# An 8 KB transfer ahead of gamma's load in an RMSNorm-and-swish kernel

## The chip, the cores and the metric

The kernel runs on one core of one Trainium2 chip. The metric is the device time of one execution in microseconds. Most executions of a kernel agree within a few tenths of a per cent; all executions compared below are of the fast state unless it is said otherwise, and the granted clock was 1.0 in every profile. "Slow" here means only that an execution took over 1.5% more than the fastest of the same kernel.

## The reference

```python
x: (16, 1024, 512) float32, gamma: (512,) float32, eps = 1e-5
rms    = np.sqrt(np.mean(x ** 2, axis=-1, keepdims=True) + eps)
x_norm = x / rms * gamma
return x_norm * (1.0 / (1.0 + np.exp(-x_norm)))
```

33.6 MB are read and 33.6 MB written.

## The kernel before

x is cut into 11 tiles of 128 partitions by 4 to 16 rows, worked on in 32 chunks of four rows. A ring of 96 rows in SBUF holds x, and the result replaces x in place. SP issues all loads, ScalarE all stores and gamma's load.

```python
sizes = [4, 4, 8] + [16] * 6 + [8, 8]
...
nc.gpsimd.memset(gamma4, 0.0).then_inc(s_zero, 1)
...
need(
    nc.scalar.dma_start(out=gamma4[0:P:32, :], in_=gamma.partition_broadcast(4)),
    s_zero, 1,
).then_inc(s_gld, 16)
nc.scalar.preload_act_table_set("silu_and_others")
stored = 0
for k in range(K + 3):
    if k < K:
        square(k)                    # ScalarE, two instructions
    while stored < T and ends[stored] <= k - 2:
        store(stored)
        stored += 1
    if 2 <= k < K + 2:
        swish(k - 2)                 # ScalarE, in place
...
for k in range(K + 1):               # VectorE
    if k < K:
        sums(k)                      # reduction of the squares
    if k == 0:
        need(nc.vector.stream_shuffle(gamma_sb, gamma4, [0] * 32), s_gld, 16
        ).then_inc(s_gamma, 1)       # gamma to all partitions
    if k == 1:
        nc.vector.wait_ge(s_gamma, 1)
    if k >= 1:
        norm(k - 1)                  # four multiplies by rstd and gamma
```

GpSimd adds eps and takes the power -0.5 between `sums` and `norm`.

## Time and profile before

| | before |
|---|---|
| median time | 160.29 us (160.28 to 160.62, 3 runs) |
| span in the profile | 160.0 us (that execution took 161.31 us) |
| VectorE / ScalarE / GpSimd busy | 87% / 78% / 41% |
| moved by DMA | 67.14 MB, 420 GB/s over the span |

### The profile page before, as it was taken

Reading aid. Unit: us, or ns where it says so; the run is one execution under the profiler, and the core shown is the slowest. Engines: PE = TensorE matmul, PEld = TensorE weight load, DVE = VectorE, ACT = ScalarE, POOL = GpSimd, SP = SyncE. Lnnn points to the kernel's source line nnn. Section 1 sums busy time; section 2 is a strip of 40 time slices with the busy share of each in tenths; the row PEclk is TensorE's granted clock in tenths of the full one; section 3 lists DMA queues with packets and bytes.
Section 4 is the critical chain, followed back from the end, with each engine's and each line's share of the span. In section 5 each row is a group of like instructions: output and inputs, shape, how many; then the busy total and the mean of one; then the engine's idle time right before and its main releaser. Section 6 shows DMA issues by size and latency. Waiting matters only on the chain.

```text
span 160.0 us, 437 instructions
## 1 busy us (share of the span) xinstructions
DVE 139.1 (87%) x162; ACT 125.1 (78%) x129; POOL 65.5 (41%) x70
## 2 busy tenths in 40 slices
DVE  0298986999999999999999999999999999999100
ACT  1839849888888889988888888888899888884400
POOL 1043552444555555444444445555554444444000
DMA  6999999989999999999999999999999999999994
GB/s 250 444 487 393 393 381 455 475 358 477 426 408 442 414 483 395 418 483 410 401 461 451 393 442 459 401 451 442 426 393 455 414 442 442 467 401 405 430 434 180
DMA packets 3179, 67.14 MB, mean 420 GB/s; under 512 B 356, under 2 KB 356, under 8 KB 360
## 3 DMA queue, kind: packets, MB, share of 16 engines
q1 hardware_dynamic: 1584, 33.56, 49.3%
q10 hardware_dynamic: 1592, 33.56, 48.8%
q14 instruction: 3, 0.02, 0.0%
HBM read 33.56 MB, written 33.55 MB: 419 GB/s over the span
## 4 chain that ended last, share of the span: by engine, by line
DVE 77%; DMA 13%; ACT 2%; issue 0%; SPq 0%; ACTq 0%
DVE xb L215 48%; DVE ms L204 29%; DMA xb<-in_x_dram 13%; ACT xb L178 1%; ACT sq L166 1%; ACT junk L159 0%; SPq L118 0%; ACTq L158 0%
## 5 line engine op out<-in xcount | busy, mean ns | idle before, releaser
L215 DVE SCALAR_TENSOR_TENSOR xb<-xb,rstd,gamma_sb 128x512 f32<-128x512 f32 x128 | 87.4, 747 | 0.0
L178 ACT ACTIVATE xb<-xb 128x2048 f32<-128x2048 f32 x32 | 61.1, 1908 | 16.3 <-DVE xb L215 16.3
L204 DVE TENSOR_REDUCE ms<-sq 128x3 f32<-128x1536 f32 x32 | 56.1, 1754 | 9.7 <-ACT sq L166 9.6
L141 POOL TENSOR_SCALAR aeps<-ms 128x4 f32<-128x4 f32 x32 | 20.7, 646 | 75.9 <-DVE ms L204 75.9
L166 ACT ACTIVATE sq<-xb 128x1536 f32<-128x1536 f32 x32 | 45.9, 1433 | 0.0
L148 POOL TENSOR_TENSOR rstd<-aeps,neg_half 128x4 f32<-128x4 f32 x32 | 44.0, 1376 | 2.7
L159 ACT ACTIVATE junk<-xb 128x512 bf16<-128x512 f32 x32 | 19.7, 615 | 5.7 <-DMA xb<-in_x_dram 5.7
L159 ACT ACTIVATION_READ_ACCUMULATOR junk<-xb 128x1 f32 x32 | 6.0, 187 | 0.0
L190 ACT ACT_TABLE_LOAD x1 | 1.3, 1283 | 3.6 <-issue 3.6
L136 POOL MEMSET gamma<- 128x512 f32 x1 | 0.5, 526 | 1.5 <-POOLq L65 1.5
L228 DVE STREAM_SHUFFLE gamma_sb<-gamma 128x512 f32<-128x512 f32 x1 | 0.7, 720 | 0.0
L255 POOL MEMSET const-float32-0.0<- 128x1 f32 x1 | 0.1, 99 | 0.2 <-issue 0.2
L255 POOL MEMSET const-bfloat16-1.0<- 128x1 bf16 x1 | 0.1, 103 | 0.0
L255 POOL MEMSET const-uint8-127<- 128x1 uint8 x1 | 0.1, 102 | 0.0
L137 POOL MEMSET neg_half<- 128x4 f32 x1 | 0.1, 102 | 0.0
L255 POOL MEMSET const-float32-1.0<- 128x1 f32 x1 | 0.1, 99 | 0.0
L228 DVE LOAD_MASK_SELECT gamma_sb<-gamma x1 | 0.0, 15 | 0.0
## 6 DMA issues: line engine op xcount, KB each, us to landing
xb<-in_x_dram SPq DMA_DIRECT2D x6, 4096.0 KB, 44.5
out_dram<-xb ACTq DMA_DIRECT2D x6, 4096.0 KB, 29.8
xb<-in_x_dram SPq DMA_DIRECT2D x3, 2048.0 KB, 38.5
out_dram<-xb ACTq DMA_DIRECT2D x3, 2048.0 KB, 11.3
xb<-in_x_dram SPq DMA_DIRECT2D x2, 1024.0 KB, 5.9
out_dram<-xb ACTq DMA_DIRECT2D x2, 1024.0 KB, 19.8
gamma<-in_gamma_dram ACTq DMA_DIRECT2D x1, 8.0 KB
```

What stands on the lines that cost most here:

```text
L136: nc.gpsimd.memset(gamma4, 0.0).then_inc(s_zero, 1)
L137: nc.gpsimd.memset(neg_half, -0.5).then_inc(s_half, 1)
L141: nc.gpsimd.tensor_scalar(out=aeps[:, k, :], in0=ms[:, k, :], scalar1=eps_f, scalar2=None, op0=ALU.add,),
L148: nc.gpsimd.tensor_tensor(out=rstd[:, k, :], in0=aeps[:, k, :], in1=neg_half, op=ALU.pow),
L159: acc = nc.scalar.activation(out=junk[k % 2], in_=xb[:, at + n_sq, :], func=AF.Square, scale=inv_d**0.5, accum_out=ms[:, k, n_sq : n_sq + 1],)
L166: square = nc.scalar.activation(out=sq[k % 2][:, 0:n_sq, :], in_=xb[:, at : at + n_sq, :], func=AF.Square, scale=inv_d**0.5,)
L178: nc.scalar.activation(out=rows, in_=rows, func=AF.Silu), s_norm, k + 1
L190: nc.scalar.preload_act_table_set("silu_and_others")
L204: nc.vector.tensor_reduce(out=ms[:, k, 0:n_sq], in_=sq[k % 2][:, 0:n_sq, :], op=ALU.add, axis=mybir.AxisListType.X,),
L215: ins = nc.vector.scalar_tensor_tensor(out=row, in0=row, scalar=rstd[:, k, j : j + 1], in1=gamma_sb, op0=ALU.mult, op1=ALU.mult,)
L228: nc.vector.stream_shuffle(gamma_sb, gamma4, [0] * 32), s_gld, 16
L255: nc = _bacc.Bacc("TRN2", target_bir_lowering=False, num_devices=1)
```

## The change

A transfer of 128 rows of 64 B from SBUF to a scratch tensor in HBM goes out from ScalarE's queue ahead of gamma's load. Nothing reads what it writes; SP waits for it at its end. As an optimization it has no purpose in the result: it puts something small in front of a load that VectorE needs early.

```diff
+    scratch = nc.dram_tensor("scratch", [P, 16], fp32, kind="Internal").ap()
+    blank = sbuf("blank", [P, 16])
...
     for t in range(early, T):
         load(t)
+    nc.sync.wait_ge(s_scratch, 16)
...
+    nc.gpsimd.memset(blank, 0.0).then_inc(s_blank, 1)
     nc.gpsimd.memset(gamma4, 0.0).then_inc(s_zero, 1)
...
+    need(nc.scalar.dma_start(out=scratch, in_=blank), s_blank, 1).then_inc(
+        s_scratch, 16
+    )
     need(
         nc.scalar.dma_start(out=gamma4[0:P:32, :], in_=gamma.partition_broadcast(4)),
```

More of the change, by code (lines that the diff above doesn't have):

```diff
@@ L81 @@
     st = [nc.alloc_semaphore(f"st{t}") for t in range(T)]
+    scratch = nc.dram_tensor("scratch", [P, 16], fp32, kind="Internal").ap()
+    blank = sbuf("blank", [P, 16])
+    s_blank = nc.alloc_semaphore("s_blank")
+    s_scratch = nc.alloc_semaphore("s_scratch")
     s_gld = nc.alloc_semaphore("s_gld")
```

## The prediction

> **What bounds the kernel now.** I read the page first (busy shares, the 40 slices), then the chain of waits, then the timeline of the first 27 us, the DMA view in narrow windows, and last the tail.
>
> From the page of the kernel before (busy time; tenths busy per fortieth of the span; the chain that ended last):
>
> ```profile
> DVE 139.1 (87%) x162; ACT 125.1 (78%) x129; POOL 65.5 (41%) x70
> ...
> DMA  6999999989999999999999999999999999999994
> ...
> DMA packets 3179, 67.14 MB, mean 420 GB/s; under 512 B 356, under 2 KB 356, under 8 KB 360
> ...
> DVE xb L215 48%; DVE ms L204 29%; DMA xb<-in_x_dram 13%; ACT xb L178 1%; ACT sq L166 1%; ACT junk L159 0%; SPq L118 0%; ACTq L158 0%
> ```
>
> The chain says: loads up to 23 us, then VectorE without a break to 148.8 us, then the last swish and a store. Taken alone that makes VectorE the bound. The DMA row says something else: it is full from the second slice to the last but one. 67.14 MB in about 157 us is 428 GB/s, and the 32 KB packets take 1.213 us each, which is 16 x 32,768 B / 1.213 us = 432 GB/s at best. So the transfers have almost no idle time either. The two meet at the end, where the second view (busy per stretch) shows the engines done and the stores still draining:
>
> ```profile
> 148.00:152.00 4.00, 0.80 (x2) 2.00 (x2) 0.00 (x0) 1.00 1.00 430
> 152.00:154.00 2.00, 0.00 (x0) 0.00 (x0) 0.00 (x0) 1.00 1.00 426
> 154.00:156.00 2.00, 0.00 (x0) 0.00 (x0) 0.00 (x0) 1.00 1.03 442
> 156.00:158.00 2.00, 0.00 (x0) 0.00 (x0) 0.00 (x0) 1.00 0.81 344
> ```
>
> (The last two columns are the DMA share and GB/s.) The last store is issued at 150.77 us and its packets start at about 152.7 us, right behind those of the store before it. The end is thus set by the drain of the stores, and compute has a little slack before it.
>
> The start, from the timeline (start, duration, engine, line):
>
> ```profile
> 1.90 0.53 POOL L136 MEMSET gamma<- 128x512 f32 x1 [1.48 <-POOLq L65]
> ...
> 2.46 1.08 ACTq L187 DMA_DIRECT2D gamma<-in_gamma_dram  x1
> 3.58 1.28 ACT L190 ACT_TABLE_LOAD   x1 [3.58 <-issue]
> ...
> 8.66 0.72 DVE L228 STREAM_SHUFFLE gamma_sb<-gamma 128x512 f32<-128x512 f32 x1
> ...
> 12.39 0.63 ACT L159 ACTIVATE junk<-xb 128x512 bf16<-128x512 f32 x1 [2.96 <-DMA xb<-in_x_dram]
> ...
> 25.25 1.76 DVE L204 TENSOR_REDUCE ms<-sq 128x3 f32<-128x1536 f32 x1 [2.04 <-ACT sq L166]
> ```
>
> Up to 25.25 us all waits are for x, and VectorE is then busy to the end. The shuffle that needs gamma comes second on VectorE, so a late gamma holds everything behind it.
>
> **What the Trainium skill says.** (1) "DMA: Bandwidth & Descriptors", section "Queues, rings and completion order": each DMA engine takes turns between the queues that have work, a packet at a time. The trace agrees: in 20 to 24 us the DMA view counts 50 packets of the load queue and 50 of the store queue, though the first are 32 KB and the second 8 KB. (2) Same page, "Why a DMA increments its semaphore by 16 and not by 1": a transfer with 128 partitions is spread over 16 engines, one with four rows over four. The trace agrees: the 356 packets under 512 B are 22 big transfers x 16 + 4 for gamma. (3) Same page, "Specifications": below 512 B a transfer costs a read-modify-write; no packet here tests that, since the only ones so small are semaphore updates (9 ns each). (4) "Perfetto Trace Analysis", section "DMA Instruction — HWDGE (DVE, Sync)": the profiled time of an issue doesn't hold the data movement. The trace agrees, and this matters here. Gamma's issue is 2.46 to 3.54 us, but no packet of its queue (q10) runs before 6.67 us:
>
> ```profile
> q1 hardware_dynamic: 66, 0.54, 127.7%
> q10 hardware_dynamic: 2, 0.00, 0.6%
> ...
> q1 hardware_dynamic: 25, 0.41, 95.5%
> q10 hardware_dynamic: 3, 0.01, 1.6%
> ...
> q1 hardware_dynamic: 23, 0.38, 87.8%
> q10 hardware_dynamic: 3, 0.00, 0.2%
> ```
>
> (windows 6 to 7, 7 to 8 and 8 to 9 us: packets, MB, share of 16 engines). The four 2 KB packets start at 6.67 to 7.56 us and the four semaphore updates at 6.76 to 8.25 us. On three engines a 16 KB load packet (0.61 us) stands between data and update. The first store shows the same 4.1 us from issue (16.31) to first packet (20.39). The x tile's last update at 6.95 us frees ScalarE at 7.37, so I add 0.4 us: gamma was usable at about 8.65 us, the moment the shuffle began.
>
> **The change, part by part.** Nothing is removed; the rest of each engine's order stays.
>
> POOL: one memset of 128x16, about 0.1 us (the 128x4 one took 102 ns), ahead of gamma's. Off the path.
>
> ScalarE's queue: one more issue. It needs only the small memset, so it starts at about 2.05 us. Issues took 1.08 us (gamma) and 0.34 to 0.36 us (stores). Gamma's own issue then moves from 2.46 to 2.5 to 3.1 us, and table load and first square by 0.1 to 0.7 us. ScalarE idles 0.42 us before chunk 1 and 2.96 us before chunk 2 waiting for x, so that is absorbed.
>
> SP: a wait for the scratch transfer, but after its last load issue (79.9 us). The transfer is over by then. Zero.
>
> DMA engines: 128 rows of 64 B plus 16 semaphore updates, 144 packets, nine per engine. 2 KB took 84 ns and 8 KB 309 ns, so about 37 ns per KB over some 9 ns: 64 B is about 11 ns (estimate from those two), 0.1 us per engine. As the end is a DMA drain, 0.1 us can show.
>
> Gamma's landing: this is the part with size. Gamma stands behind nine scratch packets in the same queue, and each takes a turn against a load packet. With the 4.1 us delay from issue, the first scratch packet comes at about 6.2 us, up to 6.7 us. Tile 2's load (16 KB packets, eight per engine) fills 6.65 to 11.9 us. One or two turns pass at the end of tile 1, the other seven or eight cost 0.61 us each: 4.3 to 4.9 us. The scratch update runs at about 10.5 to 11.5 us; gamma's data one turn later; its update another turn later, at 0.61 us or, if tile 3's 32 KB packets have begun, 1.22 us a turn. Gamma lands between 12.1 and 14.7 us (with the 0.4 us); call it 13.5, 4.8 us later than now.
>
> What that does on VectorE: from gamma's landing G to the start of chunk 4's reduction (25.25 us now) lie shuffle 0.65, three reductions of 1.67 and three groups of four multiplies of 2.65 (the steps in the chain): 0.65 + 5.0 + 7.95 = 13.6 us. It starts late only if G exceeds 25.25 - 13.6 = 11.6 us. With G = 13.5 VectorE runs 1.9 us late, for the rest of the kernel (0.5 to 3.1 us for the range of G).
>
> What that does to the end: the last store is issued at 150.77 + d. First load packets began 1.0 to 2.05 us after the first issue; with 2.05, then eight 16 KB packets (4.9 us) and 0.4 us, the end is 158.1 + d. Now it is 160.0, set by the drain (one DMA engine finishes at 159.64 us by my chaining of packets, the rest by 158.3). So d up to 1.9 us is hidden; 3.1 us would show 1.2 us. Loads aren't harmed: they wait in a full queue, tile 9's load is issued 22 us before its packets start.
>
> Sum: 0 to 1.2 us from gamma, some 0.2 us from packets and drain. 160.29 + 0.3 = 160.6 us.
>
> **The rivals.** First, all of VectorE's delay shows, as the chain of waits suggests: d of 0.5 to 3.1 us gives 160.8 to 163.4 us. For: VectorE has no gap after 25.25 us. Against: DMA is at 1.00 in the stretch in which VectorE stops. Second, gamma is hardly delayed: the 4.1 us may be a start-up of the queue which both transfers share, or small rows may travel together in one packet; then G is about 9 and the time is 160.3 to 160.4 us. For: no packet below 2 KB except updates is in this trace, so I can't see how 64 B rows are packed. Against: big rows go strictly one packet each. Third, the 64 B writes are slow to complete and gamma's update waits for them: G of 16 to 17, d about 5, 163 us or more. For: the page's remark on small writes. Against: nothing in this trace.
>
> Faster would need stores that start later to let the loads finish earlier, or the one late DMA engine to lose its 1.4 us; the bytes stay the same, so at most 1%.
>
> **Range and chances.** 2% is 3.2 us: it needs d above 5.1 us with the drain hiding 1.9, or the first rival at its upper edge. I give slower 0.05, faster 0.01, same 0.94. The range 160.1 to 162.0 us holds the main line and rival two whole, and a part of rivals one and three.
>
> **What would show it.** 500 packets under 512 B instead of 356 (128 + 16 more), the shuffle at 12 to 15 us with idle VectorE before it, chunk 4's reduction at 26 to 28 us, and a last store issued 0.5 to 3 us later while the span grows by less. A shuffle near 9 us would refute the turns; a span that grows by as much as the last issue moves would refute the slack in the drain; a shuffle after 16 us would mean that small writes cost more than turns.

## The result, and the profile after

The changed kernel took 160.12 us (median of 4 runs, 160.02 to 160.16), the kernel before 160.28 us in the same rounds. The ratio is 0.9985, with a 95% interval of 0.9968 to 1.0003. A ratio here is the mean time of one kernel's fast runs over that of the other's of the same rounds, so it isn't quite the ratio of the medians. The times are thus the same within their scatter; what there is of a difference points the other way from the predicted +0.3 us.

From the page of the changed kernel (busy time, DMA row, packets, the chain that ended last):

```profile
span 158.7 us, 439 instructions
...
DVE 138.9 (87%) x162; ACT 125.3 (79%) x129; POOL 65.4 (41%) x71
...
DMA  7999999999999999999999999999999999999997
...
q10 hardware_dynamic: 1736, 33.57, 49.3%
...
DVE xb L224 53%; DVE ms L213 32%; DMA gamma<-in_gamma_dram 5%; ACT xb L184 1%; DVE gamma_sb L237 0%; POOL gamma L142 0%; POOL blank L141 0%; POOLq L65 0%
```

ScalarE's queue (q10) has 1,736 packets instead of 1,592: 144 more, exactly 128 rows and 16 semaphore updates, so each row is a packet of its own. In the chain, gamma's load has taken the place of the x loads. Whoever reads only the chain sees a kernel that now hangs on gamma, and it isn't slower.

The start of the changed kernel, from the timeline (start, duration, engine, line):

```profile
2.04 0.35 ACTq L192 DMA_DIRECT2D scratch<-blank  x1
...
2.50 1.10 ACTq L196 DMA_DIRECT2D gamma<-in_gamma_dram  x1
...
11.04 0.72 DVE L237 STREAM_SHUFFLE gamma_sb<-gamma 128x512 f32<-128x512 f32 x1
...
18.01 0.34 ACTq L189 DMA_DIRECT2D out_dram<-xb  x1
...
22.39 0.63 ACT L165 ACTIVATE junk<-xb 128x512 bf16<-128x512 f32 x1
...
24.59 1.75 DVE L213 TENSOR_REDUCE ms<-sq 128x3 f32<-128x1536 f32 x1
```

The shuffle begins at 11.04 us instead of 8.66, after 2.26 us in which VectorE waited for gamma. The first store is issued at 18.01 us instead of 16.31. Tile 3 of x is there when ScalarE wants it at 22.39 us (no wait in front of that line), where it had waited until 23.15 us before. The reduction of chunk 4, from which on VectorE has no gap, begins at 24.59 us instead of 25.25: earlier, though gamma came later.

The DMA view of the changed kernel, 5.7 to 6.7 us and then 9.4 to 10.8 us (packets, MB, share of 16 engines):

```profile
q1 hardware_dynamic: 48, 0.39, 92.7%
q10 hardware_dynamic: 48, 0.00, 3.3%
...
q1 hardware_dynamic: 33, 0.54, 90.0%
q10 hardware_dynamic: 8, 0.01, 1.7%
```

48 load packets and 48 scratch packets in the same microsecond: strict turns, though one kind has 8 KB and the other 64 B. The packet records give the rest. A scratch packet takes 11 ns. On one DMA engine they start at 5.76, 6.08, 6.39, 6.70, 6.7 to 6.8, 7.33, 7.94 and 8.56 us, the update at 9.17 us; gamma's four packets start at 9.85 to 10.0 us and their updates at 10.54 to 10.69 us.

### The profile page after: what moved, and what is told of

It reads as the page before. It is cut to its first block, busy times and chain, and to the rows that moved or that the text cites. A ratio compares the mean times of both kernels' runs of the same rounds, so it can differ in the third digit from the quotient of the medians.

```text
span 158.7 us, 439 instructions
## 1 busy us (share of the span) xinstructions
DVE 138.9 (87%) x162; ACT 125.3 (79%) x129; POOL 65.4 (41%) x71
## 3 DMA queue, kind: packets, MB, share of 16 engines
q10 hardware_dynamic: 1736, 33.57, 49.3%
## 4 chain that ended last, share of the span: by engine, by line
DVE 85%; DMA 5%; ACT 1%; issue 1%; POOL 0%; POOLq 0%
DVE xb L224 53%; DVE ms L213 32%; DMA gamma<-in_gamma_dram 5%; ACT xb L184 1%; DVE gamma_sb L237 0%; POOL gamma L142 0%; POOL blank L141 0%; POOLq L65 0%
```

## The experiments

Two theories were put up for what sets the time. **D**: the transfers do. All bytes have to pass 16 DMA engines that are hardly ever idle, and compute has a little slack before the last store. **V**: VectorE does, as the chain of waits says, so the time moves one for one with the start of its unbroken run (chunk 4's reduction, from which on VectorE has no gap). For what delayed gamma there were three: turns in the queue, the bytes, or slow small writes to HBM.

### The changed kernel once more: after_again

No edit.

> The changed kernel once more, for a tighter interval and a second profile. Theory D (the drain of the transfers sets the end): 159.9 to 160.4 us, within 0.3 us of the kernel before, shuffle again at about 11.0 us. Theory V (the start of VectorE's unbroken run sets the end; it moved from 25.25 to 24.59 us): about 159.6 us, 0.65 us less than before.

Measured: 160.19 us (160.02 to 160.64, 6 runs), ratio 0.9989 (0.9968 to 1.001). Shuffle at 11.20 us, unbroken run from 24.96 us, last store issued at 150.49 us. As D expected; V's 159.6 us did not come. But with the start at 24.96 us, as in this profile, V would ask for only 0.3 us less than before, so this run doesn't separate the two. The profiled execution took 160.64 us, and in it one DMA engine ended at 158.94 us and the others by 158.24. That is worth keeping: in the profile before, one engine ended at 159.64 us and the others by 158.27 (161.31 us); in the first profile after, all ended by 158.30 (160.02 us). (I assigned packets to engines by chaining each start to the nearest end.) The scatter between executions is largely one late DMA engine: each of these three executions took 1.7 us longer than the time at which its last engine ended.

### Scratch behind gamma: behind

```diff
-    need(nc.scalar.dma_start(out=scratch, in_=blank), s_blank, 1).then_inc(s_scratch, 16)
     need(nc.scalar.dma_start(out=gamma4[0:P:32, :], ...), s_zero, 1).then_inc(s_gld, 16)
+    need(nc.scalar.dma_start(out=scratch, in_=blank), s_blank, 1).then_inc(s_scratch, 16)
```

> Scratch transfer issued behind gamma's instead of ahead. Both theories: shuffle back at about 8.7 us and the first store's issue back at about 16.3 us, since gamma no longer stands behind nine packets. D: 160.0 to 160.4 us, like the changed kernel. V: about 0.65 us more than the changed kernel, 160.3 us, as the unbroken run starts at about 25.2 us again. If the small writes themselves cost, this is slower than the kernel before by the same as the changed kernel.

Measured: 160.39 us (160.14 to 160.91), ratio 1.0000 (0.9976 to 1.0024). Shuffle at 9.08 us (right behind the first reduction, which ScalarE's extra issue had pushed to 7.40 us), first store at 16.20 us, unbroken run from 25.16 us. The start is that of the kernel before again, with the same 144 extra packets: the packets themselves cost nothing that shows.

### The same 8 KB in 16 rows: one_turn

```diff
-    scratch = nc.dram_tensor("scratch", [P, 16], ...); blank = sbuf("blank", [P, 16])
+    scratch = nc.dram_tensor("scratch", [16, 128], ...); blank = sbuf("blank", [16, 128])
```

> The same 8 KB ahead of gamma, but as 16 rows of 512 B: one data packet and one semaphore update on each DMA engine instead of eight and one. If the turns delay gamma: two turns instead of nine, gamma limited by its own issue again, shuffle at 8.7 to 9.3 us. If the bytes or the write to HBM delay it: shuffle at about 11 us as in the changed kernel. Time under D 160.0 to 160.4 us.

Measured: shuffle at 8.81 us, 160.49 us (160.26 to 160.81), ratio 1.0005 (0.9985 to 1.0026).

```profile
8.81 0.72 DVE L237 STREAM_SHUFFLE gamma_sb<-gamma 128x512 f32<-128x512 f32 x1
```

The same bytes, the same direction, ahead of gamma all the same, and gamma isn't late. Turns, not bytes.

### The rows read instead of written: read_in

```diff
-    need(nc.scalar.dma_start(out=scratch, in_=blank), s_blank, 1)
+    need(nc.scalar.dma_start(out=blank, in_=xf[0:P, 0:16]), s_blank, 1)
```

> The 128 rows of 64 B run the other way, from x in HBM into SBUF: no small write to HBM, the same nine packets a DMA engine ahead of gamma. If turns delay gamma: shuffle at 11.0 to 11.3 us as in the changed kernel. If the small write to HBM (read-modify-write, late confirmation) does: shuffle well before that, 9 to 10 us. Time 160.0 to 160.4 us either way.

Measured: shuffle at 11.12 us, 160.13 us (159.98 to 160.38, 4 runs), ratio 0.9988 (0.9959 to 1.0017).

```profile
11.12 0.71 DVE L236 STREAM_SHUFFLE gamma_sb<-gamma 128x512 f32<-128x512 f32 x1
```

Reads of 64 B do to gamma what writes of 64 B do, 11 ns a packet in both. Slow small writes are out.

### The first store one step later, no scratch: late_store and late_store_again

```diff
-        while stored < T and ends[stored] <= k - 2:
+        while stored < T and ends[stored] <= k - (3 if stored == 0 else 2):
```

> The kernel before without scratch, only the first store moved one step later in ScalarE's order (issue at about 22.5 to 23.5 us instead of 16.3). If the first store's packets are what slowed tile 3's load, that load lands at about 21.7 us, ScalarE's wait ends near 22.1 us and VectorE's unbroken run starts at about 24.2 us instead of 25.25. V: about 1 us faster than before, 159.2 us. D: no change, 160.0 to 160.4 us, since the same bytes have to drain.

Measured: tile 3's wait ends at 22.06 us, unbroken run from 24.16 us, both as expected; last store issued at 149.68 us; 159.89 us (159.81 to 160.48), ratio 0.9977 (0.9955 to 0.9999). The start, first of the kernel before and then of late_store:

```profile
16.31 0.36 ACTq L183 DMA_DIRECT2D out_dram<-xb  x1
...
23.15 0.63 ACT L159 ACTIVATE junk<-xb 128x512 bf16<-128x512 f32 x1 [2.32 <-DMA xb<-in_x_dram]
```

```profile
22.06 0.63 ACT L159 ACTIVATE junk<-xb 128x512 bf16<-128x512 f32 x1 [1.26 <-DMA xb<-in_x_dram]
...
24.16 1.76 DVE L204 TENSOR_REDUCE ms<-sq 128x3 f32<-128x1536 f32 x1 [0.98 <-ACT sq L166]
```

So a first store that doesn't take turns against tile 3's load does let that load land a microsecond earlier. Of V's 1 us some 0.4 us showed: V's 159.2 us is missed by 0.7, but D's "no change" (160.0 us at the least) is missed too, by 0.1.

> The kernel with the late first store and no scratch once more, to see if it beats both kernels. If its gain is real: ratio to before 0.996 to 0.999 again, about 159.9 us. If it was the draw of runs: 0.999 to 1.001.

Measured: 159.90 us (159.79 to 160.08), ratio 0.9966 (0.9948 to 0.9984). This version beats the kernel before in two sets of runs, by 0.2 to 0.3%. The changed kernel ran beside it only in the first (after_again), with a mean of 160.24 us against 160.04, which the scatter of 0.7 us doesn't settle. What the gain comes from stays open; late_busy4, below, was to show it and didn't.

### More turns ahead of gamma: plus2, plus3, plus6

A second transfer of 16, 32 or 80 rows of 64 B from the same tile, which adds 1, 2 or 5 data packets and one update on each DMA engine:

```diff
+    nc.scalar.dma_start(out=more, in_=blank[0:16, :]).then_inc(s_more, 16)   # 32, 80
     need(nc.scalar.dma_start(out=gamma4[0:P:32, :], ...), s_zero, 1).then_inc(s_gld, 16)
```

> One more scratch transfer of 16 rows ahead of gamma: two more turns a DMA engine (data, update), each 0.61 us in tile 2's load. Turns: gamma's updates at 11.75 to 11.9, shuffle at about 12.2 us, VectorE's unbroken run from about 25.8 us, last store issued at about 151.2 us. D (drain, with about 1.7 us from an issue to its packets): still hidden, 160.1 to 160.4 us. V (time follows VectorE): 1.1 us over the changed kernel, 161.2 us.

> One more scratch transfer of 32 rows: three more turns, the last of gamma's now against a 32 KB packet of tile 3 (1.21 us). Turns: shuffle at about 13.5 us, last store issued at about 152.5 us. D: the last store's packets then come after the queue has run dry, 160.6 to 161.2 us. V: 2.4 us over the changed kernel, 162.5 us.

> One more scratch transfer of 80 rows: six more turns, half of them at 1.21 us. Turns: shuffle at about 17.1 us, last store issued at about 156.2 us. D: the drain hides about 1.7 us of 6.1 us, 164.2 to 164.9 us. V: all of it shows, 166.2 us.

Measured, plus3: shuffle at 12.49 us (1 us before what I expected; gamma's updates ran before tile 3's large packets began), last store issued at 152.88 us, 161.67 us (160.79 to 162.22), ratio 1.0073 (1.0041 to 1.0105): the median is slower than D's range and faster than V's 162.5. The profiled execution is the fastest of the six, 160.79 us, and lies in D's range; what held up the others, by up to 1.4 us, no trace shows. Measured, plus6: shuffle at 15.94 us (expected 17.1), last store issued at 156.33 us, 164.00 us (163.95 to 164.03), ratio 1.0225 (1.0201 to 1.0249): 0.2 us under D's range, 2.2 under V's figure. The tail of plus6 by stretches (busy of VectorE, ScalarE, GpSimd; clock, DMA share, GB/s):

```profile
152.00:154.00 2.00, 2.00 (x4) 0.31 (x1) 0.00 (x0) 1.00 0.92 393
154.00:156.00 2.00, 0.35 (x1) 1.61 (x1) 0.00 (x0) 1.00 0.31 131
156.00:158.00 2.00, 0.00 (x0) 0.30 (x1) 0.00 (x0) 1.00 0.61 262
```

Here the queue has run dry: a DMA share of 0.31 in front of the last store. The last store's packets start at 157.17 us, 0.84 us after its issue began, and the span ends 6.4 us after that issue. With no slack left, the time follows the last store, and so VectorE.

The last store was late for a second reason as well. In plus3 and plus6 GpSimd fell into a slow state in mid-run. In the timeline of plus3, at the end:

```profile
144.14 2.78 DVE L228 SCALAR_TENSOR_TENSOR xb<-xb,rstd,gamma_sb 128x512 f32<-128x512 f32 x4
144.37 2.65 POOL L150 TENSOR_SCALAR aeps<-ms 128x4 f32<-128x4 f32 x1 [0.55 <-DVE ms L217]
...
148.17 2.74 DVE L228 SCALAR_TENSOR_TENSOR xb<-xb,rstd,gamma_sb 128x512 f32<-128x512 f32 x4 [1.24 <-POOL rstd L157]
```

The addition of eps took 2.65 us instead of 0.66, as long as VectorE's four multiplies; only the last chunk has to wait for it, 1.24 us. The Trainium skill says in "SBUF — State Buffer", section "Who interferes with whom", that a VectorE instruction with two SBUF inputs contends with a GpSimd instruction that reads SBUF, and that the port pair they share is an exclusive lock. The first addition of eps, with no multiply beside it, took 0.23 us (kernel before, at 8.83 us), and 0.66 us is about one multiply, which agrees; 2.65 us is four in a row, which the page does not explain. What tips GpSimd from one state to the other, no run settles.

Measured, plus2: shuffle at 12.43 us as expected, but 166.39 us (161.65 to 167.45); five of its six executions, the profiled one among them, count as slow (no ratio was formed), though the clock was 1.0. Two DMA engines ended at 165.7 us and the other 14 by 159.5; from 69.7 to 124.5 us, 51 of the 768 store packets of 32 KB took 1.29 to 2.1 us instead of 1.213 (2 of 768 in the kernel before), most of them on two engines by my chaining. Neither theory had this.

### What made two engines late: plus2_pad and more_behind

plus2_pad enlarges the target tensor of the extra 16 rows from 1 KB to 8 KB, to move what lies behind it in HBM; more_behind issues those 16 rows behind gamma's load:

```diff
-    more = nc.dram_tensor("more", [16, 16], ...)      # plus2_pad
+    more = nc.dram_tensor("more", [P, 16], ...)
-    nc.scalar.dma_start(out=more, in_=blank[0:16, :]).then_inc(s_more, 16)
+    nc.scalar.dma_start(out=more[0:16, :], in_=blank[0:16, :]).then_inc(s_more, 16)
```

> The kernel with the extra 16-row scratch transfer, which had two DMA engines finish 7 us after the others, with its target enlarged from 1 KB to 8 KB (the transfer is the same). If the place of the tensors in HBM made two engines slow: as the changed kernel but for the later gamma, 160.1 to 160.8 us. If the 16-row transfer itself does: 164 to 167 us again.

Measured: 166.94 us (165.32 to 167.38), ratio 1.0385 (1.0343 to 1.0427). The tail of plus2_pad by stretches:

```profile
158.00:160.00 2.00, 0.00 (x0) 0.00 (x0) 0.00 (x0) 1.00 0.31 131
160.00:162.00 2.00, 0.00 (x0) 0.00 (x0) 0.00 (x0) 1.00 0.32 139
162.00:164.00 2.00, 0.00 (x0) 0.00 (x0) 0.00 (x0) 1.00 0.27 115
```

About five of 16 engines are still at work, some 6 to 7 us long, and no compute engine is. So the size of the target isn't it; and GpSimd stayed in its fast state here (0.66 us throughout), so that isn't it either.

> The 16-row transfer that made two DMA engines late, issued behind gamma's instead of ahead of it; same packets in all, gamma at about 11 us as in the changed kernel. If the transfer itself makes engines late: 164 to 167 us. If it was the later gamma (12.2 to 12.4 us) and the order of loads and stores that follows: 160.0 to 160.4 us.

Measured: shuffle at 10.94 us, 160.09 us (160.01 to 160.53, 4 runs), ratio 0.9997 (0.9983 to 1.0012). Behind gamma the transfer is harmless. That the lateness comes from the later gamma and the order of transfers after it isn't shown: plus3 and plus6, with gamma at 12.49 and 15.94 us, didn't have it in their profiles. Its cause stays open.

### VectorE held up with no transfer changed: busy3, busy6, busy11

```diff
     need(nc.vector.stream_shuffle(gamma_sb, gamma4, [0] * 32), s_gld, 16).then_inc(s_gamma, 1)
+    for i in range(6):                       # 3, 11
+        ins = nc.vector.stream_shuffle(dummy, gamma4, [0] * 32)
+        if i:
+            need(ins, s_dummy, i)
+        ins.then_inc(s_dummy, 1)
```

> The kernel before with no scratch; VectorE does six more shuffles of 0.72 us into a spare tile right behind gamma's. No transfer changes. VectorE's unbroken run then starts at about 26.6 us (8.7 + 13.6 + 4.3) instead of 25.25 and the last store is issued at about 152.1 us. D (an issue needs 0.84 us to its first packet when the engines are free, and the drain of the store before ends at about 152.6 us): 160.0 to 160.7 us. V: 1.35 us more than before, 161.7 us. If GpSimd falls into its slow state (2.65 us for the addition of eps, as in the runs with more scratch), 1.2 us come on top of the last issue, and the time is about 161.2 us under D.

> As the run with six, with eleven more shuffles: unbroken run from about 30.4 us, last store issued at about 155.9 us. D: time = last issue + 7.7 us as in the run with six more turns, 163.6 us, so some 3.3 us of 5.1 show. V: 165.4 us. GpSimd's slow state would add 1.2 us.

Measured, busy6: unbroken run from 26.62 us, GpSimd in its slow state, last store issued at 153.47 us; 160.95 us (160.59 to 161.73), ratio 1.0035 (1.0011 to 1.006), near D's 161.2 with the slow state; V's 161.7, without it, is above. Measured, busy11: unbroken run from 30.45 us, slow state, last store issued at 157.33 us; 164.31 us, ratio 1.024 (1.0203 to 1.0277). Its four times are 163.65, 163.65, 164.96 and 165.01: the profiled one, with the slow state, is the 165.01, and the two groups lie 1.3 us apart, about the 1.24 us that the slow state costs (that the faster two were free of it is argued; they have no trace). 163.65 is D's 163.6; V's 165.4, which holds no slow GpSimd, is above all four. The issue on which the slack is read:

```profile
157.33 0.34 ACTq L185 DMA_DIRECT2D out_dram<-xb  x1
```

> The kernel before, no scratch, three shuffles of 0.72 us behind gamma's: VectorE is held 2.3 us, like the changed kernel by its late gamma. First store issued at about 18 us, unbroken run from 24.6 to 25.0 us. If the changed kernel's small gain comes from what late gamma does to the order of work: 160.0 to 160.2 us, ratio about 0.9985. If it comes from the scratch transfer itself: 160.3 to 160.5 us, ratio 1.000.

Measured: first store at 17.82 us, unbroken run from 24.86 us, both like the changed kernel, with no scratch at all; 160.25 us (159.93 to 165.44, 6 runs), ratio 1.0009 (0.9978 to 1.004). Three runs lie at 159.93 to 159.99 us, under every run of the kernel before (160.06 at the least), one at 160.51, one at 161.62, and one, counted as slow and left out of the ratio, at 165.44, as late as plus2's. The median decides nothing at this size. That a run several microseconds late came without any scratch transfer is the useful part.

### Late store, VectorE's start put back: late_busy4

The edit of late_store and four shuffles.

> The late first store with four shuffles behind gamma's: first store at about 22 to 23 us, unbroken run of VectorE at about 25.3 us as in the kernel before. If the gain of the late store comes from VectorE's earlier start (V): gone, 160.3 to 160.5 us. If it comes from the transfers (D): kept, 159.8 to 160.0 us, ratio about 0.997.

Measured: first store at 22.14 us, unbroken run from 25.14 us; 160.15 us (159.90 to 161.21), ratio 1.0007 (0.9985 to 1.0028). Inconclusive: GpSimd was in its slow state at the end of the profile and the last store was issued at 152.00 us, at the end of the slack.

### All runs by their last store

| run | last store issued, us | span of that profile, us | span minus issue |
|---|---|---|---|
| late_store_again | 149.59 | 158.5 | 8.9 |
| late_store | 149.68 | 159.2 | 9.5 |
| changed kernel | 150.11 | 158.7 | 8.6 |
| read_in | 150.15 | 158.7 | 8.6 |
| busy3 | 150.39 | 159.2 | 8.8 |
| after_again | 150.49 | 159.3 | 8.8 |
| more_behind | 150.50 | 158.8 | 8.3 |
| one_turn | 150.58 | 159.1 | 8.5 |
| behind | 150.69 | 159.4 | 8.7 |
| before | 150.77 | 160.0 | 9.2 |
| late_busy4 | 152.00 | 159.4 | 7.4 |
| plus3 | 152.88 | 159.5 | 6.6 |
| busy6 | 153.47 | 159.8 | 6.3 |
| plus6 | 156.33 | 162.7 | 6.4 |
| busy11 | 157.33 | 163.7 | 6.4 |

From 153.5 us on, the span is the last issue plus 6.3 to 6.4 us. Up to 152.0 us it is 158.5 to 159.4 us (160.0 in the one execution of the kernel before) however early the store is issued. The corner lies near 158.5 - 6.35 = 152.2 us (an estimate); the kernel before has 1.4 us of slack, the changed kernel 2.1. This is what separates D from V. Left out are plus2 (152.53, span 166.1) and plus2_pad (151.94, span 165.5), whose late DMA engines set the end: the table holds only where no engine is several microseconds late.

## Why the prediction was right or wrong

It was wrong in the sign of its small shift: +0.3 us was forecast, about -0.2 us came (ratio 0.9985 of 160.28 is 160.04, just under its low end of 160.1; the median, 160.12, is just above it). Within 2% was right and likely, but that was easy. Two steps failed: gamma's landing, forecast at 13.5 us and measured at 11.04, and the order of transfers behind it. With gamma at 11.04 us the prediction's own sum would still have given 160.29 + 0.2 = 160.5 us; it had no term that could make the kernel faster, while tile 3 came 0.76 us earlier (23.15 to 22.39) and VectorE's run 0.66 us earlier.

Right, by its own steps:
- The turns, the 144 packets, 11 ns each, and gamma behind nine of them (the turns shown by one_turn and read_in). The third rival (slow small writes) fell with read_in; the second's packing of small rows fell with the packet count.
- The threshold for VectorE, a landing of gamma 13.6 us ahead of chunk 4's reduction: 24.59 - 11.04 = 13.55 us.
- A drain that hides a delay of VectorE. The first rival (all of it shows) fell with busy11 and the table above; the change itself didn't test it, since its d was not positive.

Wrong:
- **Gamma's landing**, the term with the size: 13.5 us (12.1 to 14.7) was forecast, 11.04 us measured. The step that failed is the start of the turns. I added gamma's 4.1 us from issue to first packet to scratch's issue and got 6.2 to 6.7 us; they began at 5.76 us, 3.7 us after the issue. Gamma's own issue took 1.1 us against 0.35; counted from the issue's end the two are nearer, 3.1 us for gamma and 3.4 for scratch, but no constant either (gamma's was 2.8 to 3.8 us over the other runs without scratch ahead of it). With the earlier start four turns, not one or two, fell among tile 1's 8 KB packets at 0.31 us, one came right at the change of tiles, and only four of scratch's cost 0.61 us. I had taken the 4.1 us for a fixed latency; the last store of plus6, with idle DMA engines, needed 0.84 us. What part of it is the loads queued ahead, no run took apart.
- **d**, as a consequence: 11.04 is under the threshold of 11.6 us, so VectorE ran 0.66 us early, not 1.9 us late. The prediction did say that later stores let the loads finish earlier, but only as the way to a faster kernel, and gave it no term. It is the store's turns against tile 3's load: late gamma put the first store from 16.31 to 18.01 us; late_store moved that store alone, and tile 3's wait ended 1.1 us earlier.
- **The 0.2 us for packets and drain**: behind has the packets and a ratio of 1.0000 (0.9976 to 1.0024, so 0.2 us either way would not be seen).
- **The tail of the profile before**: one DMA engine was 1.4 us later than the rest in an execution that took 161.31 us. I built the end (158.1 + d against 160.0) on that engine and the median on other executions. Also, the 2.05 us from issue to packets was too long by more than a microsecond; measured, the end is issue + 6.35, not issue + 7.3. The two nearly cancel: a slack of 1.9 us was forecast, 1.4 us is read off the table.
- **A reading**: the 50 load packets in 20 to 24 us, called 32 KB each, are 34 of 32 KB (1.11 MB) and 16 semaphore updates. The turns hold, since an update takes one too.
- **The range**: a low end 0.2 us under the median left no room for the scatter (160.06 to 161.31 over all runs of the kernel before), and none for a gain.

Open: whether the changed kernel's 0.2 us are real. Two sets of runs agree in sign, both intervals reach 1. behind and one_turn, whose first store is early again, are at 1.000; read_in, whose start is that of the changed kernel, is at 0.9988, but more_behind, whose first store is as late (17.92 us), is at 0.9997; late_store is at 0.997. Most of this fits a small gain from the later first store, but busy3 and late_busy4 were to show it and were spoilt by late runs and by GpSimd's slow state.

## What to carry to other kernels

In these runs a small transfer cost its place in the queue, not its bytes: each row of a transfer was one turn against a packet of whatever the other queue moved, so 128 rows of 64 B (eight and an update on each engine) delayed the load behind them by 2.4 us and 16 rows of 512 B did not. Before a delay on the chain of waits is counted, look at whether the DMA engines are full to the end: here 1.4 to 2 us of VectorE's time were free, and none after that. And look at how long the profiled execution took beside the median before its tail is used as a number.

## What the Trainium skill lacked or had wrong

- "DMA: Bandwidth & Descriptors", "Queues, rings and completion order", speaks of typically 9 to 17 descriptors in a packet between two turns. Here every row was a turn of its own: 48 packets of 64 B beside 48 of 8 KB in one microsecond.
- Same page, "Specifications", gives about 0.6 us to the first byte of a transfer from SP or ScalarE. Measured from the issue's start: 0.84 us with idle engines (plus6), 3.4 to 4.9 us with loads queued from SP (scratch, gamma, first store; the 4.9 is gamma in behind). What makes the difference, no run took apart.
- Same place, the read-modify-write below 512 B is given no size: here no cost of it shows, since 64 B writes took 11 ns each, as did 64 B reads, and held gamma up equally (11.04 and 11.12 us).
- "SBUF — State Buffer", "Who interferes with whom", has the exclusive lock, but nothing on a GpSimd instruction held up by several VectorE instructions in a row; the addition of eps took 0.66 us in most runs, but 2.65 us, four multiplies long, in parts of some.
- No page gives a time for DMA engines that lag: here single engines ended 0.7 to 1.4 us late in ordinary runs, and two to five 6 to 7 us late in plus2 and plus2_pad, with store packets of up to 2.1 us (plus2) instead of 1.213.
